# Gate and up products of two feed-forward halves by seven half-sized block products, and all modulation vectors in the first half

## The chip, the cores and the metric

The kernel runs on one core of a Trainium2 chip. The metric is the time of one execution on the device in microseconds (us), median of three runs; lower is better. TensorE (PE) multiplies, VectorE (DVE), ScalarE (ACT) and GpSimd (POOL) work on vectors, and the queue of SyncE (SP) starts the transfers.

## The reference

Two layers of a transformer trunk in float32, on 512 latent tokens and 256 context tokens of width 1024. A layer is a feed-forward half, a mixer (a convolution module in the first layer, windowed attention in the second), and another feed-forward half; the last half has no context tokens. Every part is scaled and shifted by modulation vectors, which come from a condition vector for the latents and one for the context:

```
ml = silu(c) @ mod_w[i] + mod_b[i]              # nine vectors per layer; mc likewise from c_ctx
h  = rmsnorm(s) * norm_g * (1 + scale) + shift
s  = s + 0.5 * gate * ((silu(h @ w_gate) * (h @ w_up)) @ w_down)      # hidden width 2816
```

The change touches the feed-forward halves two (end of layer 0) and three (start of layer 1), both on all 768 tokens, and the place where the modulation vectors are made.

## The kernel before

Activations lie with channels on the partitions: eight tiles `xl[c]` of 128 x 512 (latents) and eight `xc[c]` of 128 x 256 (context). Each float32 operand of a product is split into two parts of a shorter type: ScalarE copies the value into the high part (`whi`, `hhi`, `hidh`), VectorE subtracts it to get the low part (`wlo`, `hlo`, `hidl`). `mm3` (L117 to 125) then issues three matmuls for each 128 x 128 block of weights: high by high, high by low, low by high, all added in PSUM.

`ffn` (L301) does a feed-forward half. It goes through the 22 hidden chunks of 128 in groups of 5, 5, 6 and 6. For each chunk it loads two weight tiles of 128 x 1024 (gate and up; `load`, L105 to 112: one transfer, one copy, one subtraction) and makes two products, each over eight chunks of input channels and in two pieces: 512 latent tokens, and 256 context tokens with 2 more columns that carry the product of the shift (258). `by_rows` (L289) multiplies the result out of PSUM by the row factor `rb`, `shift_cols` (L282) saves the two extra columns, then come silu (L318), the gating (L319) and the split into the hidden parts (L115, L116). After a group, `down` (L292) adds the group's product with the down weights to the activations (L296). In the last group the operands of the next part are made as each chunk is done (`scaled`, L225 and L226).

The root of the mean square is computed with the token sums in a column (L182), three Newton steps on GpSimd (L168 to 177) and a spreading product (L188, L194), after which ScalarE writes `rb` (L218). The products that need it are already in PSUM by then.

The modulation vectors are made in the background of `ffn` on VectorE: `mod_background` (L355) loads one 128 x 1024 tile for each of 8 chunks of a vector (`mraw`) and sums its product with the condition on the free axis (`junk`, L375), one instruction for the latents and one for the context. The first half makes the seven vectors left of layer 0 (56 tiles), the second half the nine of layer 1 (72 tiles).

PSUM has eight banks: three with the tag `a`, two `b`, two `c`, one `st`. Raw weights have three buffers, `whi` and `wlo` three each. The order on each engine is not the order of the code: a list scheduler with a cost model of its own places the instructions, by their place in the program and by when their operands and buffers are free. Once placed, each engine runs its list in order.

Of the kernel before, what the change touches and what calls it, by code (L numbers as in the profile page):

```python
# [10 lines left out]
F32 = mybir.dt.float32  # L11
# [16 lines left out]
TB = T + 2  # L28
# [6 lines left out]
GROUPS = (5, 5, 6, 6)  # L35
DVE_TAPS = ((1, 0), (2, 0), (3, 0), (4, 0))
# [6 lines left out]
# columns of the packed parameters  # L43
# [12 lines left out]
def tile_trunk(ctx: ExitStack, tc, xin, cb, cs, par, modp, modv, gu, dn, pw1, pw2, wqk, wv, wo, bv, rpb, out):  # L56
# [25 lines left out]
    sT = const.tile([P, NC, 32], F32, name="sT")  # L82
    cst = const.tile([P, NC, 2], F32, name="cst")
    nc.sync.dma_start(cst, cs)
# [20 lines left out]
    def load(src, cols=1024):  # L105
        raw = main.tile([P, 1024], F32, tag="raw", name="raw", bufs=3)
# [11 lines left out]
    def mm3(po, w, acts, o, n, first=True, last=True):  # L118
        whi, wlo = w
        k = len(acts)  # L120
        for i, (ah, al) in enumerate(acts):
            s = slice(i * P, (i + 1) * P)
            nc.tensor.matmul(po, lhsT=whi[:, s], rhs=ah[:, o:o + n], start=first and i == 0, stop=False)  # L123
            nc.tensor.matmul(po, lhsT=whi[:, s], rhs=al[:, o:o + n], start=False, stop=False)  # L124
            nc.tensor.matmul(po, lhsT=wlo[:, s], rhs=ah[:, o:o + n], start=False, stop=last and i == k - 1)  # L125

    def h_tiles(i):
        return (main.tile([P, TB], F32R, tag="hhi", name=f"hhi{i}", bufs=8),
                main.tile([P, TB], F32R, tag="hlo", name=f"hlo{i}", bufs=8))

# [14 lines left out]
    def both(ap):  # L145
        return ap.rearrange("p (s c) -> p s c", s=1).broadcast_to([P, 2, NC])

    def finish_mod(l, n, bias=None):
        t = mods[l, n]
        nc.vector.tensor_tensor(t, t, both(pv("mod_b", (l * 9 + n) * 8, 8)), ALU.add)  # L150
        if n % 3 == 1:
            d = derv[l, n] = derived(l, n)
            nc.vector.scalar_tensor_tensor(d, t, 1.0, both(pv("norm_g", (l * 3 + n // 3) * 8, 8)), ALU.add, ALU.mult)
        elif n in (2, 8):
            d = derv[l, n] = derived(l, n)
            nc.vector.tensor_scalar(d, t, 0.5, None, ALU.mult)
        elif n == 5:
            d = derv[l, n] = derived(l, n)
            nc.vector.tensor_tensor(d, t, both(pv("b_pw2" if l == 0 else "b_o")), ALU.mult)

# [1 line left out]
    def newton_rsqrt(sums, k, eps, quick):  # L162
        """1 / sqrt(sums / D + eps) of the columns, from a guess by the exponent."""
# [20 lines left out]
    def spread(y, streams, use):  # L184
        """Token values on partitions to rows on all partitions."""
# [25 lines left out]
    def rms_rows(streams, quick=False):  # L211
# [6 lines left out]
        spread(y, streams, lambda q, o, n: nc.scalar.activation(rb[:, o:o + n], q, AF.Copy))  # L218
# [41 lines left out]
    # products of one unit of weights: (first token, tokens, columns, stream) of each piece; the last  # L260
    # one holds the products of the shift as well
# [38 lines left out]
    def ffn(idx, h, hid, pieces, gate, bg, done, pre=(), tail=None):  # L300
        f0 = 0  # L301
        e = pieces[-1][0] + pieces[-1][1]
        for gi, gn in enumerate(GROUPS):
            hids = []
            for j in range(gn):
                f = f0 + j
                wg, wu = (pre[2 * f + i] if 2 * f + i < len(pre) else load(gu[idx, f, i]) for i in range(2))
# [15 lines left out]
                bg()  # L323
# [15 lines left out]
            for d in range(NC):  # L339
# [4 lines left out]
                if last:  # L344
                    done(d)
                elif d % 3 == 1:
                    bg()
            f0 += gn

# [7 lines left out]
    def mod_background(pool, units):  # L357
# [5 lines left out]
        def step(k):  # L363
            for _ in range(k):
# [8 lines left out]
                for s in range(2):  # L373
# [22 lines left out]
    # ================= layer 0, first half =================  # L396
    with tc.tile_pool(name="start", bufs=1) as hid:
        nc.gpsimd.memset(sT, 0.0)
# [59 lines left out]
    with tc.tile_pool(name="ffn0", bufs=1) as hid:  # L458
        step = mod_background(hid, unit_list(0, range(2, 9)))
        hn = new_h()  # L460
        ffn(0, h, hid, FULL, (0, 2), lambda: step(2),
# [5 lines left out]
    # ================= layer 0, convolution module =================  # L467
    with tc.tile_pool(name="conv", bufs=1) as cv:
# [47 lines left out]
        # taps on the tensor engine: four shifts of 32 channels on the partitions, four such products side by side  # L516
# [19 lines left out]
        # sums over the channels, shifted by the mean of the first 128 of them  # L536
# [87 lines left out]
        ln_out(z, mps, CTX)  # L624
        for d in range(NC):
# [18 lines left out]
        h = new_h()  # L644
        scaled_all(h, derv[0, 7], mods[0, 6])
        rms_rows(BOTH)
        ctx2.close()

    # ================= layer 0, second half; layer 1, first half =================
    with tc.tile_pool(name="ffn1", bufs=1) as hid:  # L650
        step = mod_background(hid, unit_list(1, range(9)))
        hn = new_h()
        ffn(1, h, hid, FULL, (0, 8), lambda: step(3),
            lambda d: scaled_parts(hn, d, BOTH, derv[1, 1], mods[1, 0]))
        rms_rows(BOTH)
        step(99)
        h = hn
        hn = new_h()

        def tail(st):  # L660
            rms_rows((st,), True)
# [279 lines left out]
```

## Time and profile before

| | |
|---|---|
| median of three runs | 2747.97 us (2747.5 to 2748.68) |
| span of the profiled execution, first to last instruction | 2745.9 us |
| TensorE busy | 2700.0 us (98%), 16948 matmuls, as many weight loads |
| VectorE busy | 1673.2 us (61%) |
| ScalarE busy | 822.1 us (30%) |
| transfers | 277.73 MB, mean 101 GB/s |

The profile gives the span alone for its execution, and no other time of it; the median lies 2.07 us above the span. The trace records for each instruction its start, its duration, what it reads and writes, and for an engine that was idle what it waited for. Matmuls overlap, so that their durations do not add up; what one costs in a stream is read from the distance of starts. By the column sums that end each part, half one runs to about 600 us, the convolution module to 897 us, half two to 1449 us, half three to 2020 us and attention to 2361 us.

### The profile page before, as it was taken

The numbers are of one execution on the slowest core, as the hardware profiler recorded it, in microseconds if no ns is written. First come the engines' busy times: TensorE is split into PE (matmuls) and PEld (weight loads), VectorE is DVE, ScalarE is ACT, GpSimd is POOL, SyncE is SP. The second block draws the span as 40 slices with busy tenths as digits, with TensorE's granted clock in tenths as the row PEclk, the third lists the DMA queues.
The fourth block names the chain that finished last, engine by engine and source line by source line (L and its number), as shares of the span: only waits on it lengthen the run. The fifth ranks groups of instructions, "written<-read, shape, count | busy, mean of one in ns | idle before, by whom it ended". The sixth has DMA issues, their size and how long they took to land.

```text
span 2745.9 us, 41215 instructions
## 1 busy us (share of the span) xinstructions
PE 2700.0 (98%) x16948; PEld 2353.4 (86%) x16948; DVE 1673.2 (61%) x3048; ACT 822.1 (30%) x1306; POOL 68.1 (2%) x124
## 2 busy tenths in 40 slices
PE   8999999999989999999999999999999999999997
PEld 4888888888869888888888888888888888999997
DVE  5999533357998999833363433433478576544446
ACT  4212221241236212121242221212346455422224
POOL 0000000011020100000000000000000000000001
PEclk9999999999999999999999999999999999999999
DMA  8565212122435565412121212121242121233223
GB/s 297 163 211 175 88 55 71 56 71 78 127 78 178 168 195 177 158 54 70 58 72 50 75 50 67 61 69 61 80 121 62 58 73 46 74 105 95 88 99 112
DMA packets 95101, 277.73 MB, mean 101 GB/s; under 512 B 11329, under 2 KB 25793, under 8 KB 94657
## 3 DMA queue, kind: packets, MB, share of 16 engines
q1 hardware_dynamic: 94336, 273.52, 31.4%
q8 instruction: 133, 2.18, 0.3%
q0 software_dynamic: 576, 1.57, 0.2%
q14 instruction: 56, 0.45, 0.1%
HBM read 269.09 MB, written 4.38 MB: 100 GB/s over the span
## 4 chain that ended last, share of the span: by engine, by line
PE 93%; DVE 3%; ACT 1%; issue 1%; DMA 1%; POOL 0%; SPq 0%; DVEq 0%; POOLq 0%; ACTq 0%
PE a L125 12%; PE a L123 12%; PE a L124 11%; PE c L123 9%; PE c L125 9%; PE c L124 9%; PE b L125 8%; PE b L124 8%; PE b L123 8%; PE st L793 2%; PE b L784 1%; DVE y L514 1%; PE c L532 1%; PE a L759 1%; PE a L760 1%
## 5 line engine op out<-in xcount | busy, mean ns | idle before, releaser
L110 ACT ACTIVATE whi<-raw 128x1024 fp32r<-128x1024 f32 (+2 forms) x376 | 360.0, 960 | 1437.8 <-PE c L124 1046.0
L111 DVE TENSOR_TENSOR wlo<-raw,whi 128x1024 fp32r<-128x1024 f32 (+2 forms) x376 | 411.8, 1098 | 100.1 <-ACT whi L110 98.1
L125 PE MATMUL a<-hhi,wlo 128*128 128x512 f32 (+2 forms) x1264 | 442.2, 350 | 0.4 <-DVE wlo L111 0.4
L124 PE MATMUL a<-hlo,whi 128*128 128x512 f32 (+2 forms) x1264 | 440.3, 348 | 0.0
L123 PE MATMUL a<-hhi,whi 128*128 128x512 f32 (+2 forms) x1264 | 440.3, 349 | 0.0
L123 PE MATMUL c<-hhi,whi 128*128 128x258 f32 (+2 forms) x1456 | 428.6, 295 | 4.3 <-ACT hhi L115 2.1
L125 PE MATMUL c<-hhi,wlo 128*128 128x258 f32 (+2 forms) x1456 | 429.2, 295 | 0.0
L124 PE MATMUL c<-hlo,whi 128*128 128x258 f32 (+2 forms) x1456 | 427.1, 294 | 0.5 <-DVE hlo L116 0.5
L375 DVE SCALAR_TENSOR_TENSOR junk<-mraw,sbc 128x1024 f32<-128x1024 f32 x256 | 312.7, 1221 | 3.8 <-ACT sbc L360 2.0
L123 PEld LDWEIGHTS c<-hhi,whi 128*128 128x128 f32 x1456 | 275.7, 190 | 15.6 <-ACT hhi L115 2.7
L123 PE MATMUL b<-hhi,whi 128*128 128x512 f32 (+2 forms) x800 | 280.3, 350 | 6.0 <-ACT hhi L225 3.4
L124 PEld LDWEIGHTS c<-hlo,whi 128*128 128x128 f32 x1456 | 276.7, 190 | 10.8 <-DVE hlo L116 1.3
L125 PE MATMUL b<-hhi,wlo 128*128 128x512 f32 (+2 forms) x800 | 280.9, 351 | 0.5 <-DVE wlo L111 0.5
L125 PEld LDWEIGHTS c<-hhi,wlo 128*128 128x128 f32 x1456 | 275.1, 189 | 7.1 <-issue 1.0
L124 PE MATMUL b<-hlo,whi 128*128 128x512 f32 (+2 forms) x800 | 280.1, 350 | 0.5 <-DVE hlo L226 0.5
L125 PEld LDWEIGHTS a<-hhi,wlo 128*128 128x128 f32 x1264 | 237.8, 188 | 34.0 <-issue 1.1
L124 PEld LDWEIGHTS a<-hlo,whi 128*128 128x128 f32 x1264 | 238.1, 188 | 32.9 <-issue 0.2
L123 PEld LDWEIGHTS a<-hhi,whi 128*128 128x128 f32 x1264 | 238.0, 188 | 31.3 <-issue 0.8
L123 PEld LDWEIGHTS b<-hhi,whi 128*128 128x128 f32 x800 | 151.0, 189 | 29.6 <-ACT hhi L225 3.6
L124 PEld LDWEIGHTS b<-hlo,whi 128*128 128x128 f32 x800 | 151.0, 189 | 22.8 <-DVE hlo L226 1.0
L125 PEld LDWEIGHTS b<-hhi,wlo 128*128 128x128 f32 x800 | 150.9, 189 | 22.2 <-DVE wlo L111 1.0
L124 PE MATMUL a<-hidl,whi 128*128 128x512 f32 (+1 forms) x431 | 162.7, 377 | 0.0
(202 smaller groups left out, 4169.8 us busy)
## 6 DMA issues: line engine op xcount, KB each, us to landing
raw<-in_gu SPq DMA_DIRECT2D x176, 512.0 KB
mraw<-in_modv SPq DMA_DIRECT2D x128, 512.0 KB
raw<-in_dn SPq DMA_DIRECT2D x80, 384.0 KB
raw<-in_dn SPq DMA_DIRECT2D x64, 320.0 KB
raw<-in_pw SPq DMA_DIRECT2D x24, 512.0 KB
us<-v SPq DMA_DIRECT2D x64, 142.0 KB
mraw<-in_modp SPq DMA_DIRECT2D x16, 512.0 KB
raw<-in_wqk SPq DMA_DIRECT2D x16, 512.0 KB
```

The lines of the kernel that those rows point to most:

```text
L110: nc.scalar.activation(hi[:, :cols], raw[:, :cols], AF.Copy)
L111: nc.vector.tensor_tensor(lo[:, :cols], raw[:, :cols], hi[:, :cols].bitcast(F32), ALU.subtract)
L123: nc.tensor.matmul(po, lhsT=whi[:, s], rhs=ah[:, o:o + n], start=first and i == 0, stop=False)
L124: nc.tensor.matmul(po, lhsT=whi[:, s], rhs=al[:, o:o + n], start=False, stop=False)
L125: nc.tensor.matmul(po, lhsT=wlo[:, s], rhs=ah[:, o:o + n], start=False, stop=last and i == k - 1)
L375: nc.vector.scalar_tensor_tensor(junk, raw, 1.0, sbc[:, s, :], ALU.mult, ALU.mult, accum_out=m[:, s, c:c + 1])
L514: nc.vector.scalar_tensor_tensor(yo, u[:, k:k + n], w, yo, ALU.mult, ALU.add)
L532: nc.tensor.matmul(po[ST * g:ST * g + ST, e:e + PIECE], lhsT=dg[:, 4 * m + g], rhs=t[:, g, 4 * m:4 * m + PIECE], start=m == 0, stop=m == 7)
L759: nc.tensor.matmul(so, lhsT=qq[:, qsl], rhs=kk[:, ks], start=True, stop=False)
L760: nc.tensor.matmul(so, lhsT=ql[:, qsl], rhs=kk[:, ks], start=False, stop=True)
L784: nc.tensor.transpose(pt[:, i * P:(i + 1) * P], p[:, i * P:(i + 1) * P], ident)
L793: nc.tensor.matmul(po[64 * a:64 * a + 64, :P], lhsT=v[:, c0:c0 + 64], rhs=PT[a][:, i * P:(i + 1) * P], start=i == 0, stop=i == 3)
```

## The change

In the halves two and three the gate and up products are no longer made block by block. The 768 tokens are taken as two blocks of 384 (256 latents and 128 context tokens each, with two columns for the shift: 386), the eight chunks of input channels as four even and four odd ones, the hidden chunks as pairs. The product of a pair is then one of 2 x 2 blocks by 2 x 2 blocks, and is made with seven block products instead of eight (Winograd's form): four sums of the weight quarters, four of the activation quarters, and additions of the products.

- `s_weights` loads the two tiles of a pair, makes the four weight sums on VectorE (new L398 to L402) and splits seven quarters in four pieces: quarters (1, 2), (6, 5) and (7, 3) together, (4) alone. Each takes one of the three `whi` and `wlo` buffers.
- `s_unit` makes the seven products (L417), each of 4 x 3 matmuls of 386 columns, in the order 1, 2, 6, 5, 7, 3, 4. Products 1, 6, 7 and 4 add up in one bank (`a`), 5 and 3 in another (`c`), 2 stands alone (`b`). ScalarE saves three sums in between (`kept`, L422) and writes one row (L439), VectorE writes three rows (L429, L435, L437) into a tile in SBUF.
- The row factor (L487, L498), silu (L489) and gating (L500) then work on these tiles.
- `s_prepare` makes the activation quarters and their sums for two chunks of channels at a time: four scalings on ScalarE into `sg`, two copies on GpSimd, seven quarters split in four pieces, four subtractions into `tu`. The tiles `sg` and `tu` have one buffer each. The quarters take 16 slots with the tag `h` and 12 with the tag `hx`; the input of the convolution's last product, `z`, fills all 16 of `h`.
- `s_ffn` runs over pairs in groups of 2, 2, 2, 2 and 3, so that there are 40 down steps of a half in place of 32. The down products read the same columns as before.
- All 128 modulation tiles are made in half one; for four vectors of layer 1 the context is left out, since the last half has no context tokens.
- Raw weights have four buffers.

```diff
-GROUPS = (5, 5, 6, 6)            # still used by halves one and four
+PAIRS = (2, 2, 2, 2, 3)
+    def s_weights(src, pool):
+        raws = []
+        for i in range(2):
+            raw = main.tile([P, 1024], F32, tag="raw", name="raw", bufs=4)
+            nc.sync.dma_start(raw, src[i])
+            raws.append(raw)
+        q = [raws[0][:, :512], raws[0][:, 512:], raws[1][:, 512:], raws[1][:, :512]]
...
+        def parts_of(t, names):
+            n = 512 * len(names)
+            hi = main.tile([P, 1024], F32R, tag="whi", name="whi", bufs=3)
+            lo = main.tile([P, 1024], F32R, tag="wlo", name="wlo", bufs=3)
+            split(hi[:, :n], lo[:, :n], t[:, :n])
...
+        parts_of(raws[0], (1, 2))
+        nc.vector.tensor_tensor(s1, q[2], q[3], ALU.add)
+        nc.vector.tensor_tensor(s2, s1, q[0], ALU.subtract)
+        parts_of(s12, (6, 5))
+        nc.vector.tensor_tensor(s3, q[0], q[2], ALU.subtract)
+        nc.vector.tensor_tensor(s4, q[1], s2, ALU.subtract)
+        parts_of(s34, (7, 3))
+        parts_of(raws[1], (4,))
+    def s_unit(src, hs, pool, row):
+        made = s_weights(src, pool)
+        def product(name, p, first):
+            hi, lo, o = made[name]
+            for j in range(4):
+                k = slice(o + j * P, o + j * P + P)
+                ah, al = hs[name][j]
+                for i, (a, b) in enumerate(((hi, ah), (hi, al), (lo, ah))):
+                    nc.tensor.matmul(p, lhsT=a[:, k], rhs=b, ...)
+        x, y, z = (bank(t)[:, :SB] for t in "abc")
+        product(1, x, True)
+        a = kept(x)
+        product(2, y, True)
+        nc.vector.tensor_tensor(row[:, 0, 0], y, a, ALU.add)
+        product(6, x, False)
+        b = kept(x)
+        product(5, z, True)
+        d = kept(z)
+        product(7, x, False)
+        nc.vector.tensor_tensor(row[:, 1, 1], x, d, ALU.add)
+        product(3, z, False)
+        nc.vector.tensor_tensor(row[:, 0, 1], z, b, ALU.add)
+        product(4, x, False)
+        nc.scalar.activation(row[:, 1, 0], x, AF.Copy)
+    def s_prepare(j, hs, pool, A, B):
+        sx = s_row(pool, "sg")                               # bufs=1
+        tt = s_row(pool, "tu").rearrange("p a b n -> p (a b) n")
...
+        split(*hs[1][j], sx[:, 0, 0])
+        two((2, 3), sx[:, 1])
+        nc.vector.tensor_tensor(tt[:, 0], sx[:, 0, 1], sx[:, 0, 0], ALU.subtract)
+        nc.vector.tensor_tensor(tt[:, 1], sx[:, 1, 1], tt[:, 0], ALU.subtract)
+        two((5, 6), tt[:, :2])
+        nc.vector.tensor_tensor(tt[:, 2], sx[:, 1, 1], sx[:, 0, 1], ALU.subtract)
+        nc.vector.tensor_tensor(tt[:, 3], sx[:, 1, 0], tt[:, 1], ALU.subtract)
+        two((7, 4), tt[:, 2:])
-        step = mod_background(hid, unit_list(0, range(2, 9)))
+        step = mod_background(hid, unit_list(0, range(2, 9)) + unit_list(1, range(9)))
-        ffn(0, h, hid, FULL, (0, 2), lambda: step(2), ...)
+        ffn(0, h, hid, FULL, (0, 2), step, ...)              # bg(3) per hidden chunk, bg(2) per down step
-        h = new_h()
-        scaled_all(h, derv[0, 7], mods[0, 6])
-        rms_rows(BOTH)
-        step = mod_background(hid, unit_list(1, range(9)))
-        ffn(1, h, hid, FULL, (0, 8), lambda: step(3), ...)
+            if d % 2:                                        # inside the loop of the last conv product
+                s_prepare(d // 2, hs, hid, derv[0, 7], mods[0, 6])
+        s_rows(BOTH)
+        s_ffn(1, hs, hid, (0, 8), done=done)
+        s_ffn(2, hs2, hid, (1, 2), tail=tail)
```

Three places of the new order. The first is TensorE in half two. Before, from one weight tile to the next (names: `h..3` is a channel chunk, `whi_13233` a gate tile, `whi_13239` the up tile of the same hidden chunk, `whi_13363` the gate tile of the next):

```order
L123 MATMUL c_13295<-hhi7_8133,whi_13233 128x258
L124 MATMUL c_13295<-hlo7_8134,whi_13233 128x258
L125 MATMUL c_13295<-hhi7_8133,wlo_13234 128x258
L123 MATMUL c_13320<-hhi0_8119,whi_13239 128x258
L124 MATMUL c_13320<-hlo0_8120,whi_13239 128x258
L125 MATMUL c_13320<-hhi0_8119,wlo_13240 128x258
```

Now, at the end of product 6 of a gate tile pair (`whi_9648` holds quarters 6 and 5, `whi_9654` 7 and 3, `whi_9771` 1 and 2 of the up weights that come next):

```order
L417 MATMUL a_9662<-h_8518,whi_9648 128x386
L417 MATMUL a_9662<-h_8519,whi_9648 128x386
L417 MATMUL a_9662<-h_8518,wlo_9649 128x386
L417 MATMUL a_9791<-h_7840,whi_9771 128x386
L417 MATMUL a_9791<-h_7841,whi_9771 128x386
L417 MATMUL b_9792<-hx_7844,whi_9771 128x386
L417 MATMUL b_9792<-hx_7845,whi_9771 128x386
L417 MATMUL a_9662<-hx_7856,whi_9654 128x386
```

Four matmuls with the next weights stand between product 6 and product 7, in 22 units of the 44. The second place is ScalarE beside it (`kept_9704` saves the bank after product 6, `kept_9718` after product 5):

```order
L422 ACTIVATE kept_9677<-a_9662 128x386
L115 ACTIVATE hid_9620<-tu_9367 128x768
L115 ACTIVATE whi_9658<-raw_9638 128x512
L115 ACTIVATE whi_9771<-raw_9765 128x1024
L422 ACTIVATE kept_9704<-a_9662 128x386
L422 ACTIVATE kept_9718<-c_9664 128x386
```

The copy of the next weights stands ahead of the two that save the banks. Its buffer is that of `whi_9648`, the third before it.

The third place is VectorE where half two begins, after the convolution's last product. Before (`x7`, `xc7`: the last channel chunk; `hlo`: low parts of the operand; `junk`: modulation):

```order
L636 TENSOR_TENSOR t_7924<-x7_82,t_7978 128x4x8x8
L640 TENSOR_TENSOR xc7_95<-xc7_95,t_8006 128x256
L116 TENSOR_TENSOR hlo4_8025<-mod0_6_2647,hhi4_8024 128x2
L226 SCALAR_TENSOR_TENSOR hlo5_8027<-xc5_93,dv0_7_3625,hhi5_8026 128x256
L375 SCALAR_TENSOR_TENSOR junk_8722,mod1_1_8577<-mraw_8718,sbc_8116 128x1024
L116 TENSOR_TENSOR hlo5_8027<-mod0_6_2647,hhi5_8026 128x2
L226 SCALAR_TENSOR_TENSOR hlo6_8029<-xc6_94,dv0_7_3625,hhi6_8028 128x256
```

Now (`sg` and `tu` with a number are the single buffers of one call of `s_prepare`: 7832 the first call, 8056 the second; `h` and `hx` the low parts):

```order
L116 TENSOR_TENSOR h_7841<-sg_7832,h_7840 128x386
L469 TENSOR_TENSOR tu_8057<-sg_8056 128x386
L470 TENSOR_TENSOR tu_8057<-sg_8056,tu_8057 128x386
L472 TENSOR_TENSOR tu_8057<-sg_8056 128x386
L473 TENSOR_TENSOR tu_8057<-sg_8056,tu_8057 128x386
L116 TENSOR_TENSOR wlo_8579<-s34_8565,whi_8578 128x1024
L822 TENSOR_TENSOR xc7_92<-xc7_92,t_8492 128x256
L221 TENSOR_TENSOR acc_80<-acc_80,t_8496 128x512
L116 TENSOR_TENSOR h_7841<-sg_8056,h_7840 128x386
```

The second, third and fourth call of `s_prepare` stand one behind the other after the convolution's last product, the first call's tile being free only when its first quarter has a slot of `h`. From the first row shown to the low parts of quarters 5 and 6 of the last call there are 32 rows on VectorE.

## Rows read from the trace of the kernel before

**Rows 1.** page, busy time of each engine: us, share of the span, instructions

```profile
PE 2700.0 (98%) x16948; PEld 2353.4 (86%) x16948; DVE 1673.2 (61%) x3048; ACT 822.1 (30%) x1306; POOL 68.1 (2%) x124
```

**Rows 2.** page, chain that ended last, by engine

```profile
PE 93%; DVE 3%; ACT 1%; issue 1%; DMA 1%; POOL 0%; SPq 0%; DVEq 0%; POOLq 0%; ACTq 0%
```

**Rows 3.** timeline, TensorE: start us, us, operation; the first of each stretch

```profile
1302.57 0.29 PE L123 MATMUL c<-hhi,whi 128*128 128x258 f32 x1
...
1308.33 0.39 PE L123 MATMUL b<-hhi,whi 128*128 128x512 f32 x1
...
1313.91 0.40 PE L123 MATMUL a<-hhi,whi 128*128 128x512 f32 x1
```

**Rows 4.** groups of instructions by shape: busy us, mean ns, idle before

```profile
L375 DVE SCALAR_TENSOR_TENSOR junk<-mraw,sbc 128x1024 f32<-128x1024 f32 x256 | 312.7, 1221 | 3.8 <-ACT sbc L360 2.0
...
L111 DVE TENSOR_TENSOR wlo<-raw,whi 128x1024 fp32r<-128x1024 f32 x232 | 283.7, 1223 | 86.3 <-ACT whi L110 84.6
...
L125 PEld LDWEIGHTS c<-hhi,wlo 128*128 128x128 f32 x1456 | 275.1, 189 | 7.1 <-issue 1.0
L110 ACT ACTIVATE whi<-raw 128x1024 fp32r<-128x1024 f32 x232 | 245.7, 1060 | 982.3 <-PE c L124 733.8 <-PE b L124 76.4 <-PE a L124 75.7
...
L319 DVE SCALAR_TENSOR_TENSOR tu<-tu,bcol,sg 128x512 f32<-128x512 f32 x88 | 66.2, 752 | 7.5 <-ACT whi L110 0.5 <-ACT sg L318 0.4
L116 DVE TENSOR_TENSOR hidl<-tu,hidh 128x768 fp32r<-128x768 f32 x66 | 63.0, 954 | 2.1 <-ACT hidh L115 1.6
...
L786 ACT ACTIVATE pts<-b 128x512 f32<-128x512 f32 x64 | 37.6, 596 | 56.7 <-PE b L784 56.5
...
L319 DVE SCALAR_TENSOR_TENSOR tu<-tu,bcol,sg 128x256 f32<-128x256 f32 x66 | 31.7, 480 | 0.0
L289 DVE TENSOR_TENSOR sg<-c,rb 128x256 f32<-128x256 f32 x74 | 31.4, 425 | 107.9 <-PE c L125 106.2 <-ACT rb L218 1.7
...
L209 DVE TENSOR_TENSOR acc<-acc,t 128x512 f32<-128x512 f32 x42 | 29.0, 692 | 13.1 <-ACT t L208 12.9
...
L375 DVE DVE_READ_ACCUMULATOR junk<-mraw,sbc 128x1 f32 x256 | 21.9, 85 | 0.0
```

**Rows 5.** windows: stretch, its us, busy of PE, PEld, DVE, ACT, POOL, clock, DMA share, GB/s

```profile
100.00:300.00 200.00, 200.00 (x1143) 175.44 (x1143) 185.24 (x323) 39.77 (x51) 0.00 (x0) 1.00 0.56 181
300.00:500.00 200.00, 200.00 (x1144) 175.26 (x1143) 78.22 (x123) 42.63 (x53) 0.00 (x0) 1.00 0.20 64
1450.00:1500.00 50.00, 50.00 (x285) 43.42 (x285) 20.84 (x35) 12.93 (x17) 2.57 (x13) 1.00 0.15 49
1500.00:1900.00 400.00, 400.00 (x2283) 350.60 (x2282) 154.12 (x243) 80.25 (x102) 0.00 (x0) 1.00 0.20 63
1990.00:2050.00 60.00, 57.83 (x299) 48.25 (x298) 46.25 (x94) 24.99 (x39) 3.28 (x6) 1.00 0.36 110
```

**Rows 6.** timeline, TensorE, where the second feed-forward half begins

```profile
919.03 0.39 PE L123 MATMUL c<-hhi,whi 128*128 128x258 f32 x1 [2.10 <-DVE bcol L282]
...
920.44 0.42 PE L124 MATMUL c<-hlo,whi 128*128 128x258 f32 x1
...
923.45 0.36 PE L123 MATMUL c<-hhi,whi 128*128 128x258 f32 x1
```

**Rows 7.** timeline, GpSimd, the reciprocal roots of that place

```profile
904.04 1.05 POOL L177 TENSOR_TENSOR nwt<-nwt 128x6 f32<-128x6 f32 x1
905.17 0.20 POOL L170 TENSOR_TENSOR nwt<-nwt 128x6 f32<-128x6 f32 x1
```

**Rows 8.** waits of TensorE from 560 to 2050 us: total, times, longest

```profile
PE c L123 <- DVE bcol L282: 2.1, 1, 2.1
PE b L724 <- ACT hhi L252: 1.5, 1, 1.5
```

More of the change, by code (lines that the diff above doesn't have):

```diff
@@ L122, in mm3, with slot @@
             s = slice(i * P, (i + 1) * P)
-            nc.tensor.matmul(po, lhsT=whi[:, s], rhs=ah[:, o:o + n], start=first and i == 0, stop=False)
-            nc.tensor.matmul(po, lhsT=whi[:, s], rhs=al[:, o:o + n], start=False, stop=False)
-            nc.tensor.matmul(po, lhsT=wlo[:, s], rhs=ah[:, o:o + n], start=False, stop=last and i == k - 1)
+            if o is not None:
+                ah, al = ah[:, o:o + n], al[:, o:o + n]
+            nc.tensor.matmul(po, lhsT=whi[:, s], rhs=ah, start=first and i == 0, stop=False)
+            nc.tensor.matmul(po, lhsT=whi[:, s], rhs=al, start=False, stop=False)
+            nc.tensor.matmul(po, lhsT=wlo[:, s], rhs=ah, start=False, stop=last and i == k - 1)
+    def slot(pool=None):
+        if pool is None:
+            return main.tile([P, TB], F32R, tag="h", name="h", bufs=2 * NC)
+        return pool.tile([P, TB], F32R, tag="hx", name="hx", bufs=12)
     def h_tiles(i):
-        return (main.tile([P, TB], F32R, tag="hhi", name=f"hhi{i}", bufs=8),
-                main.tile([P, TB], F32R, tag="hlo", name=f"hlo{i}", bufs=8))
+        return slot(), slot()
     mods = {}
@@ L306, in ffn @@
                 f = f0 + j
-                wg, wu = (pre[2 * f + i] if 2 * f + i < len(pre) else load(gu[idx, f, i]) for i in range(2))
+                wg, wu = (pre[2 * f + i] if 2 * f + i < len(pre) else load(gu[idx // 3, f, i]) for i in range(2))
                 hh = hid.tile([P, T], F32R, tag="hidh", name="hidh", bufs=6)
@@ new lines, in s_unit, with kept @@
+    def s_unit(src, hs, pool, row):
[6 more added lines that the diff above has]
+                for i, (a, b) in enumerate(((hi, ah), (hi, al), (lo, ah))):
+                    nc.tensor.matmul(p, lhsT=a[:, k], rhs=b, start=first and j == 0 and i == 0,
+                                     stop=j == 3 and i == 2, skip_group_check=True)
+        def kept(p):
+            t = pool.tile([P, SB], F32, tag="kept", name="kept", bufs=3)
+            nc.scalar.activation(t, p, AF.Copy)
+            return t
+        x, y, z = (bank(t)[:, :SB] for t in "abc")
[13 more added lines that the diff above has]
+        nc.scalar.activation(row[:, 1, 0], x, AF.Copy)
@@ L372, in step @@
                 m = mods[l, n]
-                for s in range(2):
+                for s in range(mod_streams(l, n)):
                     junk = pool.tile([P, 1024], F32, tag="junk", name="junk", bufs=1)
@@ L624, in tile_trunk @@
         ln_out(z, mps, CTX)
+        ctx2.close()
+    with tc.tile_pool(name="ffn12", bufs=1) as hid:
+        hs = {}
         for d in range(NC):
@@ L905, in _layout @@
     gate, up, down = (i[k].reshape(4, *i[k].shape[2:]) for k in ("ffn_w_gate", "ffn_w_up", "ffn_w_down"))
-    g["gu"] = np.stack([np.stack([_tiles(gate[k]), _tiles(up[k])], axis=1) for k in range(4)])
+    g["gu"] = np.stack([np.stack([_tiles(gate[k]), _tiles(up[k])], axis=1) for k in (0, 3)])
+    g["gs"] = np.stack([np.stack([_quarters(gate[k]), _quarters(up[k])], axis=1) for k in (1, 2)])
     g["dn"] = np.stack([_tiles(down[k]) for k in range(4)])
```

147 lines of the change are left out of this document (117 added, 30 removed).

## The prediction

> **What bounds the kernel now.** I read the busy times first, then the chain of waits, then the timeline of TensorE, then the windows. TensorE is busy for 2700.0 of 2745.9 us [rows 1], and the chain that ended last lies on it for 93% [rows 2]. Busy TensorE is not TensorE at its peak, so the reader should look at the distance of starts: from 1302.57 to 1308.33 us stand 48 matmuls of 258 columns, 0.1200 us each, and from there to 1313.91 us 24 of 512 columns, 0.2325 us each [rows 3]. The cost follows the columns: 254 more take 0.1125 us more, 0.000443 us per column. In halves two and three TensorE is busy for all of the stretch from 1500 to 1900 us, with the clock at 1.00 (2.4 GHz) [rows 5]. So the time there is a number of columns, and taking columns away shortens it, as long as the other engines keep up. From 1500 to 1900 us VectorE is busy for 154 of 400 us and ScalarE for 80 [rows 5]: there is room, but the change uses most of it.
>
> **TensorE, what goes and what comes.** A half has 22 hidden chunks, 2 products each, 8 channel chunks, 3 matmuls, in two pieces: 1056 matmuls of 512 columns and 1056 of 258. In two halves that is 2112 x (0.2325 + 0.1200) = 744.5 us. Now a half has 11 pairs, 2 units each, 7 products of 4 x 3 matmuls of 386 columns, in two halves 3696. On the line through the two measured points one takes 0.1200 + 128 x 0.000443 = 0.1767 us, together 653.1 us. The difference is -91.4 us, or 33.8 us for a pair before and 29.7 us now. The down products read the same columns in two runs in place of one. No row shows that form; I take it at 0, between 0 and 5% of the 371 us that 2 x 528 x (0.2325 + 0.1190) us make, 19 us.
>
> The weight loads speak against this sum. A load takes 189 ns [rows 4], longer than the 177 ns that I give to a matmul of 386 columns, and the loads are busy for 86% of the span [rows 1]. The Trainium skill (Perfetto Trace Analysis, Identifying the Most-Contended Engine) says to judge TensorE's headroom by the busy share of weight loads and not by that of matmuls. By that the new matmuls would cost their loads, 698.5 us in place of 653.1. The trace speaks against it: 48 matmuls with a load of 189 ns each start every 120 ns [rows 3, 4], so loads overlap one another.
>
> **VectorE in a pair.** From the rows of the same shapes (386 columns between 0.425 and 0.692 us, so 0.56) [rows 4]: six low parts of 1024 columns and two of 512, 8.7 us; eight weight sums of 512, 5.5; six rows out of PSUM, 3.4; four row-factor products of 768, 3.8; gating, 2 x (0.752 + 0.480) = 2.5; two hidden low parts, 1.9. That is 25.8 us in 29.7 us of TensorE: 87%, where the kernel before has 39% [rows 5]. It fits, but with little slack, and nothing on it is background work that could wait.
>
> **The wait in a pair.** The order shows a place where TensorE must stop. The weights' three buffers are used in turn by four pieces, so the first piece of the next unit takes the buffer of quarters 6 and 5 and can be copied only when both products are done. In the 22 units where product 5 comes ahead of product 6, four matmuls that want this copy stand directly behind product 6, and on ScalarE the copy stands ahead of the one that saves the bank for product 7. So TensorE waits for one copy of 1024 columns, 1.06 us [rows 4], and its start. Twenty of these units lie outside the two transitions below: 20 x 1.1 = +22 us. Bounds: 0, if the buffer is free early enough, and 20 x (1.06 + 1.22) = 46 us, if the low part is waited for as well. In the other 22 units product 5 ends after product 6 and ten of its matmuls (1.8 us) cover the save, and product 7 (2.1 us) covers the copy; I take 0.
>
> **The transitions.** Where half two begins, `s_prepare` is called four times with single buffers, and the first call waits for a slot that the convolution's last product holds. So three calls run one after the other behind that product. From the first low part to the low parts of quarters 5 and 6 of the last call VectorE has 32 instructions: sixteen of 386 columns (9.0 us), eight of 772 and one of 768 (8.6), one of 1024 (1.2), three of 512 (2.1), and small ones of 1.1, in all 22 us. TensorE has for that time 24 matmuls of 256 columns (2.9 us) and three products (6.4 us), and then stops, some 13 us; one more for the first copy, 14. Before, the same place cost a wait of 2.10 us and a spell at 0.5 of the clock (1.2 GHz), with starts 0.215 us apart instead of 0.120 from 920.44 to 923.45 us [rows 6]. Such a spell of 3.4 us loses 1.7 us. I take two spells: 14 + 3.4 - 3.8 = +14 us, bounds 0 and 25.
>
> GpSimd's root steps stand in this path too: they took 1.05 us each while VectorE worked and 0.20 us when it stood idle [rows 7]. The Trainium skill (SBUF — State Buffer, Who interferes with whom) says that a VectorE instruction with two inputs in SBUF contends with a GpSimd instruction that reads SBUF, and the two durations agree with it. The upper bound holds the ten steps at the longer time.
>
> Where half three begins, the first three calls have slots early and only the last is late. Before, TensorE did not wait there: 50.00 of 50 us [rows 5]. From the last update to the low parts of quarters 5 and 6 VectorE now has 12.5 us by the same rows, TensorE four products' worth, 8 us, and the spreading product then waits for GpSimd, some 1.5 us: +6, and one spell, +8 us; bounds 0 and 14. In the eight inner group ends of these halves the last hidden parts are late by about what three prepared down steps cover; I take 0.5 us each, +4, bounds 0 and 16.
>
> **The modulation vectors.** Half one gets 72 more tiles: its instructions go from 112 to 224, each 1.221 + 0.085 us [rows 4], 293 us in all. With the 39% of VectorE's other work over some 560 us (218 us) it is busy for 91%. From 100 to 300 us it was busy for 185 of 200 us with the same mix, and TensorE for all 200, with the transfers at 0.56 [rows 5]. Queue SP holds the same alternation of weights and tiles as there, only for longer. So 0, with 10 us as the price if the cover fails at the group ends; the last of these instructions stands in the last group, ahead of the convolution. What half two loses of them gives TensorE nothing, except at its start, where they stood in the path, which is in the 3.8 us.
>
> **Sum.** -91.4 + 22 + 14 + 8 + 4 = -43.4 us, so a span of 2702.5 us. The median of the runs shown lies 2.07 us above the span of before (2747.97 to 2745.9), and I add the same: 2704.6, say 2705 us.
>
> **Rivals.**
> - *The waits do not come, or half of them.* For it: VectorE at 93% left TensorE without a wait [rows 5]. Against: the order puts the copy right behind product 6. Without the 22 and the 4 us: 2679 us; chance 0.17.
> - *The clock falls at each wait.* For it: the wait of 2.10 us was followed by 1.2 GHz [rows 6]. Against: a wait of 1.5 us where attention starts (L724) [rows 8] left the clock at 1.00 in the stretch to 2050 us [rows 5]. Twenty spells at 1.7 us: 2705 + 34 = 2739 us; chance 0.10. The Trainium skill (TensorE: Matmul & The Clock Gate, A second HAM failure mode: psum-queue depth-cycling) tells of short idle times between groups of matmuls that made the clock swing; no run here shows it yet.
> - *Slower: VectorE cannot keep up in either unit of a pair.* Its list has waits in it (rows that need a product stand ahead of low parts that TensorE needs), and at 87% it cannot catch up. The price is 1.06 + 1.22 us in each of 44 units, 100 us in place of 22: 2705 + 78 = 2783 us. It decides from 1.6 us per unit on: 44 x 1.6 - 22 = 48 us, which brings 2705 to 2753. Against: the down steps in between give it 4.2 us of TensorE for two updates and a low part of 512 columns, 1.9 us. Chance 0.11.
> - *Each new matmul costs its weight load:* 3696 x 0.189 = 698.5 us in place of 653.1, so 45 us come back: 2750 us, no change. For it: the load is longer than the new matmul [rows 4]. Against: the starts 120 ns apart [rows 3]. Chance 0.03. It is what the Trainium skill's rule on weight loads would make of this kernel (Perfetto Trace Analysis, above).
>
> **Chances.** The forecast 0.59, the rivals 0.17, 0.10, 0.11 and 0.03. Its own range, from the bounds of the pair and of the first transition, is 2684 to 2732 us. The range for all reaches to the first two rivals and leaves the others out: 2676 to 2740 us. A measurement of this kernel can tell 0.2% (5.5 us) from no change. Faster by more than that (under 2742.5): 0.85; within it 0.05; slower 0.10.
>
> **What would show it.** Starts of 386-column matmuls 0.177 us apart; 22 waits of about 1.1 us of TensorE for `whi` of the new split; a gap of some 14 us where half two begins, and of 6 us at half three; TensorE without waits in half one, VectorE over 90% to about 520 us. Wrong would be: starts above 0.185 us, waits in all units, the clock at half inside the halves, or TensorE waiting in half one.

## The result, and the profile after

The changed kernel takes 2699.39 us (median of 4 runs, 2698.88 to 2700.21), beside 2747.8 us for the kernel before on the same chip (4 runs, 2747.5 to 2748.68): a ratio of 0.9822, 95% interval 0.9808 to 0.9836. The forecast was 2705 us, the range 2676 to 2740 us. The profiled execution has a span of 2698.4 us at a mean granted clock of 0.992.

The busy times and the chain by engine answer to [rows 1, 2]. TensorE's busy time has gone from 2700.0 to 2629.3 us, VectorE's up by 232 us, and the chain has moved a little from TensorE to VectorE.

```profile
PE 2629.3 (97%) x16420; PEld 2358.1 (87%) x16420; DVE 1905.2 (71%) x3268; ACT 985.1 (37%) x1601; POOL 77.5 (3%) x140
...
PE 90%; DVE 4%; issue 2%; ACT 2%; DMA 1%; POOL 1%; SPq 0%; DVEq 0%; POOLq 0%; ACTq 0%
```

The timeline of TensorE in half two shows the new stream and its stop (start us, us, operation, in brackets the idle time before and what ended it). From 1027.03 to 1029.15 us stand the 12 matmuls of product 5, then the 12 of product 6, the last at 1031.08.

```profile
1027.03 0.52 PE L417 MATMUL c<-hx,whi 128*128 128x386 f32 x2
...
1029.15 0.51 PE L417 MATMUL a<-hx,whi 128*128 128x386 f32 x2
...
1031.08 0.34 PE L417 MATMUL a<-h,wlo 128*128 128x386 f32 x1
1032.44 0.62 PE L417 MATMUL a<-h,whi 128*128 128x386 f32 x2 [1.02 <-ACT whi L115]
1032.89 0.51 PE L417 MATMUL b<-hx,whi 128*128 128x386 f32 x2
1033.24 0.52 PE L417 MATMUL a<-hx,whi 128*128 128x386 f32 x2
```

Twelve matmuls in 2.12 us are 0.1767 us each, the value read off the line through [rows 3]. A weight load still takes 190 ns, longer than that (groups of instructions: busy us, mean ns, idle before):

```profile
L417 PEld LDWEIGHTS a<-h,whi 128*128 128x128 f32 x880 | 160.0, 190 | 30.9 <-ACT whi L115 26.2
```

ScalarE's timeline at the same place shows what TensorE waits for: the copy of the next unit's first weights starts as product 6 ends, and the save of product 6's bank stands behind it.

```profile
1027.39 0.63 ACT L115 ACTIVATE whi<-raw 128x512 fp32r<-128x512 f32 x1
1031.33 1.06 ACT L115 ACTIVATE whi<-raw 128x1024 fp32r<-128x1024 f32 x1 [3.31 <-issue]
1032.29 0.48 ACT L422 ACTIVATE kept<-a 128x386 f32<-128x386 f32 x1
```

In the waits of TensorE from 905 to 1960 us this is nearly the only row (total us, times, longest):

```profile
PE a L417 <- ACT whi L115: 19.5, 21, 1.0
PE st L206 <- DVE t L200: 1.3, 1, 1.3
```

The windows answer to [rows 5] (same columns); the two from 905 to 1960 us leave out only the start of half three, and the last two are the places where halves two and three begin.

```profile
100.00:300.00 200.00, 200.00 (x1146) 175.74 (x1145) 187.86 (x328) 39.76 (x51) 0.00 (x0) 1.00 0.59 192
300.00:500.00 200.00, 200.00 (x1145) 175.50 (x1144) 186.76 (x328) 42.65 (x53) 0.00 (x0) 1.00 0.64 213
...
905.00:1425.00 520.00, 509.76 (x2881) 482.48 (x2880) 355.61 (x504) 206.04 (x322) 4.91 (x8) 1.00 0.22 67
1436.00:1960.00 524.00, 513.47 (x2889) 483.10 (x2888) 352.58 (x499) 198.41 (x302) 0.60 (x3) 1.00 0.23 73
1500.00:1900.00 400.00, 391.73 (x2216) 372.83 (x2216) 266.35 (x373) 146.73 (x225) 0.00 (x0) 1.00 0.22 69
...
880.00:910.00 30.00, 23.14 (x93) 17.06 (x92) 22.86 (x36) 20.47 (x35) 8.18 (x18) 0.77 0.11 35
1420.00:1450.00 30.00, 27.72 (x147) 25.84 (x146) 23.77 (x36) 17.82 (x29) 7.59 (x15) 0.94 0.11 36
```

Half one holds VectorE at 93% without a wait of TensorE. Inside half three the clock is 1.00 and the idle time 8.27 us, all of it the waits above. Where half two begins, TensorE is busy for 23.14 of 30 us at a mean clock of 0.77; its rows there answer to [rows 6]:

```profile
884.23 0.45 PE L417 MATMUL a<-h,whi 128*128 128x386 f32 x1 [1.75 <-ACT h L115]
...
888.11 0.69 PE L417 MATMUL b<-hx,whi 128*128 128x386 f32 x1 [0.78 <-DVE hx L116]
...
897.36 2.04 PE L206 MATMUL st<-t,ones 128*128 128x512 f32 x2 [1.83 <-DVE t L200]
...
899.52 0.53 PE L417 MATMUL b<-h,whi 128*128 128x386 f32 x1
...
902.45 0.45 PE L417 MATMUL c<-h,whi 128*128 128x386 f32 x1 [0.52 <-DVE h L116]
```

A matmul of 386 columns shows 0.34 us at clock 1.00 and 0.53 us at 0.50 (1.2 GHz). The long form stands from 886.9 to 900.6 us, after TensorE had worked in short pieces between waits; it ends while TensorE still waits for operands.

To size the steps I add up, over the timeline, the distance from each start to the next less the time that its columns take (0.1767, 0.2325 and 0.1185 us for 386, 512 and 256), and call the rest the lost time. It counts waits, restarts and half clock together, and is good to about 1 us for a place.

### The profile page after: what moved, and what is told of

It reads as the page before. It is cut to its first block, busy times and chain, and to the rows that moved or that the text cites. A ratio compares the mean times of both kernels' runs of the same rounds, so it can differ in the third digit from the quotient of the medians.

```text
span 2698.4 us, 40901 instructions
## 1 busy us (share of the span) xinstructions
PE 2629.3 (97%) x16420; PEld 2358.1 (87%) x16420; DVE 1905.2 (71%) x3268; ACT 985.1 (37%) x1601; POOL 77.5 (3%) x140
## 4 chain that ended last, share of the span: by engine, by line
PE 90%; DVE 4%; issue 2%; ACT 2%; DMA 1%; POOL 1%; SPq 0%; DVEq 0%; POOLq 0%; ACTq 0%
PE a L417 13%; PE a L125 8%; PE a L127 8%; PE a L126 8%; PE c L417 6%; PE c L125 6%; PE c L126 6%; PE c L127 6%; PE b L125 5%; PE b L126 5%; PE b L127 5%; PE b L417 3%; PE st L975 2%; PE b L966 1%; DVE y L691 1%
## 5 line engine op out<-in xcount | busy, mean ns | idle before, releaser
L110 ACT ACTIVATE whi<-raw 128x1024 fp32r<-128x1024 f32 (+3 forms) x304 | 270.0, 891 | 862.2 <-PE c L126 454.3
L111 DVE TENSOR_TENSOR wlo<-raw,whi 128x1024 fp32r<-128x1024 f32 (+3 forms) x304 | 306.0, 1009 | 89.8 <-ACT whi L110 87.7
L125 PE MATMUL a<-h,whi 128*128 128x512 f32 (+2 forms) x826 | 270.0, 328 | 1.1 <-DVE sg L301 1.1
L127 PE MATMUL a<-h,wlo 128*128 128x512 f32 (+2 forms) x826 | 269.0, 326 | 0.9 <-DVE wlo L111 0.9
L126 PE MATMUL a<-h,whi 128*128 128x512 f32 (+2 forms) x826 | 269.0, 326 | 0.0
L417 PE MATMUL a<-h,whi 128*128 128x386 f32 x880 | 234.8, 345 | 21.9 <-ACT whi L115 19.5
L125 PE MATMUL c<-h,whi 128*128 128x258 f32 (+2 forms) x768 | 233.1, 306 | 1.2 <-ACT h L115 1.1
L126 PE MATMUL c<-h,whi 128*128 128x258 f32 (+2 forms) x768 | 233.3, 305 | 0.6 <-DVE h L116 0.6
L127 PE MATMUL c<-h,wlo 128*128 128x258 f32 (+2 forms) x768 | 232.4, 303 | 0.0
L417 PEld LDWEIGHTS a<-h,whi 128*128 128x128 f32 x880 | 160.0, 190 | 30.9 <-ACT whi L115 26.2
L125 PE MATMUL b<-h,whi 128*128 128x512 f32 (+2 forms) x550 | 181.7, 330 | 5.3 <-ACT h L237 3.4
L126 PE MATMUL b<-h,whi 128*128 128x512 f32 (+2 forms) x550 | 180.8, 329 | 0.5 <-DVE h L238 0.5
L125 PEld LDWEIGHTS a<-h,whi 128*128 128x128 f32 x826 | 155.8, 189 | 16.9 <-DVE sg L301 2.0
L126 PEld LDWEIGHTS a<-h,whi 128*128 128x128 f32 x826 | 156.2, 189 | 14.1 <-issue 0.8
L126 PEld LDWEIGHTS c<-h,whi 128*128 128x128 f32 x768 | 145.3, 189 | 8.6 <-DVE h L116 1.2
L125 PEld LDWEIGHTS c<-h,whi 128*128 128x128 f32 x768 | 144.1, 188 | 9.6 <-ACT h L115 1.5
L417 PE MATMUL a<-h,wlo 128*128 128x386 f32 x440 | 149.4, 340 | 0.0
```

The lines of the kernel that those rows point to most:

```text
L110: nc.scalar.activation(hi[:, :cols], raw[:, :cols], AF.Copy)
L111: nc.vector.tensor_tensor(lo[:, :cols], raw[:, :cols], hi[:, :cols].bitcast(F32), ALU.subtract)
L125: nc.tensor.matmul(po, lhsT=whi[:, s], rhs=ah, start=first and i == 0, stop=False)
L126: nc.tensor.matmul(po, lhsT=whi[:, s], rhs=al, start=False, stop=False)
L127: nc.tensor.matmul(po, lhsT=wlo[:, s], rhs=ah, start=False, stop=last and i == k - 1)
L417: nc.tensor.matmul(p, lhsT=a[:, k], rhs=b, start=first and j == 0 and i == 0, stop=j == 3 and i == 2, skip_group_check=True)
```

## Experiments

All times are medians beside the kernel before on the same chip (2748.1 to 2748.5 us there). Where two kernels were not run together, their ratios to it are compared.

**1. Three raw buffers again.** Edit, in `load` and `s_weights`:

```
-        raw = main.tile([P, 1024], F32, tag="raw", name="raw", bufs=4)
+        raw = main.tile([P, 1024], F32, tag="raw", name="raw", bufs=3)
```

> The changed kernel with three raw weight buffers in place of four (undoes that part of the change). Theory: the transfers land long before they are used, so 2699 us, within 4 us; the waits for the copy behind product 6 stay, 21 times about 1 us. Rival: half a unit of prefetch is gone, and TensorE or VectorE waits for transfers, at 1 us or more in each of 44 units: 2740 us or more, with DMA named in the waits.

2695.87 us, ratio 0.9809 (0.9796 to 0.9823). In halves two and three no transfer is waited for, and the waits for the copy stay:

```profile
PE a L417 <- ACT whi L115: 18.5, 20, 1.0
```

The fourth buffer buys nothing. The 3.5 us less are not told from nothing, since the two kernels did not run together and their intervals overlap. In the traces they gather in small steps: about 1 us before half two, 1.2 us in halves two and three, where one wait for the copy is gone, and about 1 us behind them; the rest of the cause is open.

**2. Quarter 4 in a buffer of its own.** On top of the first edit, in `parts_of` (the low part likewise, as `w4l`):

```
-            hi = main.tile([P, 1024], F32R, tag="whi", name="whi", bufs=3)
+            hi = pool.tile([P, 512], F32R, tag="w4h", name="w4h", bufs=1) if n == 512 else main.tile(...)
```

> Three raw buffers, and the fourth piece of a unit's weights (quarter 4 alone) in a buffer of its own, so that the ring of three turns once per unit and the first piece of the next unit takes the buffer of quarters 1 and 2, which is free early. Theory: the 21 waits of 0.8 to 1.0 us behind product 6 came from that ring; they go, and with their restart (about 1.1 us each in the distances of starts) 22 us with them: 2676 us if three raw buffers cost nothing. Rival: the copy was only named last, and the save of the bank (0.48 us) or a low part on VectorE is next: half or more of the waits stay, 2688 us or more.

2674.17 us, ratio 0.9730 (0.9717 to 0.9743), 21.7 us under experiment 1 on the same chip. From 905 to 1400 us the view of waits is empty, and the window that had 8.27 us of idle time has none:

```profile
1500.00:1900.00 400.00, 400.00 (x2237) 380.55 (x2236) 273.24 (x378) 155.77 (x234) 0.00 (x0) 1.00 0.22 70
```

In the place of the copy, ScalarE's timeline has only the save behind product 6, and TensorE doesn't notice it:

```profile
1028.30 0.85 ACT L115 ACTIVATE hid<-tu 128x768 fp32r<-128x768 f32 x1 [0.56 <-DVE tu L500]
1031.05 0.49 ACT L422 ACTIVATE kept<-a 128x386 f32<-128x386 f32 x1 [1.91 <-PE a L417]
```

So the ring of three made the waits, as the forecast read it from the order, and they cost what it said.

**3. Early slots for the first operand chunks.** In `s_prepare`:

```
-            ones_ = [slot() for _ in range(2)]
+            ones_ = [slot(of) for _ in range(2)]
-        two((7, 4), tt[:, 2:])
+        two((7, 4), tt[:, 2:], None if j == 1 else of)      # `two` takes the pool
```

> The changed kernel, with the first two operand chunks of a half in the 12 slots that the convolution does not hold (the last two parts of chunk 1 go to the others instead), so that the first preparation and most of the second run before the convolution's last product. Theory: VectorE's list behind that product is shorter by 8 us of its 22, and TensorE stops that much less: 2691 us (2688 to 2695), and the spell at half clock is shorter than 13.65 us. Rival: the column sums, GpSimd's root steps and the spreading product set the end of the gap, so at most 3 us are saved: 2696 us or more.

2689.68 us, ratio 0.9786 (0.9773 to 0.9799): 9.7 us less than the kernel after, and 6.2 us less than experiment 1, which ran on the same chip. The window where half two begins is now

```profile
880.00:910.00 30.00, 27.26 (x135) 25.13 (x134) 23.98 (x37) 17.86 (x30) 8.18 (x15) 0.89 0.11 36
```

and the lost time of that place falls from 15.5 to 9.3 us, by the 6.2 us that the comparison on one chip gives. One wait for the copy is gone here too (20, 18.5 us), which is 1 us of the rest; the other 2.5 us are less than the intervals of two chips tell apart. So VectorE's list sets the end of the gap and the rival is refuted, but the gain is nearer to 6 us than to the 8 that were expected.

**4. The modulation vectors alone,** on the kernel before:

```
-        step = mod_background(hid, unit_list(0, range(2, 9)))
+        step = mod_background(hid, unit_list(0, range(2, 9)) + unit_list(1, range(9)))
...
-        ffn(1, h, hid, FULL, (0, 8), lambda: step(3),
+        ffn(1, h, hid, FULL, (0, 8), nothing,
```

> The kernel before, with all modulation vectors made in the first half and nothing else changed. Theory: VectorE has the room in half one (over 90% busy there, TensorE never waiting), and half two loses only the wait and the half-clock spell at its start, so 2744 to 2748 us. Rival: the cover fails at the group ends of half one, and the end of half one or the convolution is later by 10 us: 2758 us.

2744.59 us, ratio 0.9986 (0.9977 to 0.9995). VectorE is busy for 93% from 300 to 500 us and for 95% from there to 600 us, and TensorE is never idle there, although this kernel makes all 256 sums in half one where the change leaves 32 out; where half two begins TensorE is busy for 60.00 of 60 us, where it had the wait and the spell of [rows 6].

```profile
300.00:500.00 200.00, 200.00 (x1143) 175.29 (x1142) 185.92 (x327) 42.64 (x53) 0.00 (x0) 1.00 0.58 191
500.00:600.00 100.00, 100.00 (x574) 87.86 (x573) 95.16 (x176) 34.56 (x63) 0.00 (x0) 1.00 0.52 167
880.00:940.00 60.00, 60.00 (x339) 51.98 (x338) 32.39 (x63) 23.54 (x43) 3.53 (x13) 1.00 0.17 55
```

**5. Experiments 2 and 3 together.**

> The two edits together: quarter 4 in a buffer of its own with three raw buffers, and the early slots for the first two operand chunks. Theory: they act at different places, so their gains add: 2674.2 less the 9.7 us that the slots gave alone, 2664.5 us, within 4 us. Rival: with the ring changed the first weights come later into the transition, so that half or less of the 9.7 us is left: 2669 us or more.

2666.25 us, ratio 0.9702 (0.9687 to 0.9716). The gains add to within 2 us, whether the slots are taken at 9.7 us (2664.5 us) or at 6.2 (2668 us). From 1000 to 1350 us TensorE is busy for all of the time; what is lost lies in the transitions, 7.8 us at half two and 7.0 at half three.

**6 and 7. More work for VectorE,** on experiment 2. In `s_weights` (five times in the second):

```
-        nc.vector.tensor_tensor(s3, q[0], q[2], ALU.subtract)
+        for _ in range(3): nc.vector.tensor_tensor(s3, q[0], q[2], ALU.subtract)
```

> On the kernel with quarter 4 in its own buffer: the third sum of each unit is computed three times in place of once (same result), two more VectorE instructions of 512 columns, 0.6 us each, in all 44 units, 53 us of VectorE work. Theory: TensorE's stream sets the time, and a pair's VectorE list grows from 25.8 to 28.3 us of 29.7: 2674 to 2680 us. Rival (the one that forecast a slower kernel): waits inside VectorE's list leave no slack, and each unit is later by what is added, 44 times 1.2 us: 2727 us.

> As the one with the sum computed three times, but five times: four more instructions in each unit, 106 us of VectorE work, a pair's list 30.7 us. Theory: now the list is longer than TensorE's 29.7 us and VectorE sets the time of a pair, 22 times 1 us more and something for the waits in the list: 2690 to 2715 us. Rival 1: the down steps between the pairs give it a lead, nothing is seen: under 2682 us. Rival 2: no slack at all, 44 times 2.4 us: 2780 us.

2678.16 us, ratio 0.9746 (0.9731 to 0.9760), and 2679.55 us, ratio 0.9751 (0.9736 to 0.9765). The second expectation fails: the 106 us of added work (VectorE's busy time goes from 1904.3 to 2004.1 us) cost 5.4 us beside experiment 2; the two ran on different chips, and their intervals allow for 0 to 13 us. TensorE doesn't wait in the window

```profile
1000.00:1350.00 350.00, 350.00 (x1990) 337.00 (x1989) 276.92 (x400) 136.75 (x208) 0.00 (x0) 1.00 0.21 68
```

The reason is in VectorE's timeline of the second kernel (start us, us):

```profile
1005.95 0.68 DVE L401 TENSOR_TENSOR s<-raw 128x512 f32<-128x512 f32 x1
1006.55 0.68 DVE L402 TENSOR_TENSOR s<-raw,s 128x512 f32<-128x512 f32 x1
1007.15 0.68 DVE L401 TENSOR_TENSOR s<-raw 128x512 f32<-128x512 f32 x1
```

Instructions that follow one another without a wait start 0.60 us apart where each shows 0.68 us. VectorE's durations overlap by some 0.08 us and do not add up, as TensorE's do not. By the distances of starts (1.14, 0.60 and 0.47 us for 1024, 512 and 386 columns, 0.88 for 768, 0.66 and 0.40 for the two parts of the gating) the list of a pair is 23.1 us and not 25.8, and with eight sums more it is 27.9 us, still less than TensorE's 29.7. So the list never got longer than TensorE's, and this experiment doesn't show what happens when it does. What the added work costs is lost in the transitions, which go from 14.4 and 6.9 us in experiment 2 to 17.5 and 10.8 us.

**8. One product less,** on experiment 2: `product(4, x, False)` is left out.

> On the kernel with quarter 4 in its own buffer: the matmuls of the last of the seven products are left out in all units (the lower left block of each unit then lacks that product, and the output is not the reference's). 528 matmuls of 386 columns less, 93.3 us at 0.1767 us each. Theory: TensorE needs 25.4 us for a pair then, VectorE 25.8, so VectorE becomes the bound and some of the gain is lost: 2584 to 2610 us. Rival: matmuls cost their weight load, 0.189 us, so 99.8 us go and VectorE hides: 2574 us. Rival 2: VectorE was near its limit already, and half or less of the 93 us comes: 2627 us or more.

2601.13 us, ratio 0.9464 (0.9449 to 0.9480), 73 us less of the 93.3. The time lies in the expected interval, but not for the reason given. VectorE is busy for 74%, and TensorE waits at the inner group ends for the last hidden parts, in the stretch from 905 to 1400 us four times:

```profile
PE a L125 <- ACT hid L115: 3.5, 2, 1.7
PE b L125 <- ACT hid L115: 3.5, 2, 1.7
PE a L417 <- ACT h L115: 1.7, 1, 1.7
```

Over both halves eight such waits are 14.0 of the 21.0 us more of lost time. One of the eight was followed by half clock inside half two (mean 0.83 from 1040 to 1050 us). It is the way from the last product to the down step that is late, not the sum of VectorE's work.

**9. Matmuls that fill the gap,** on the kernel after, at the end of `s_prepare`:

```
+        if j == 3 and B is mods[0, 6]:
+            for jj in range(4):
+                pf = pst()[:, :SB]
+                for _ in range(6):
+                    nc.tensor.matmul(pf, lhsT=hs[1][jj][0][:, :P], rhs=hs[1][jj][0], start=True, stop=True)
```

> The changed kernel, with 24 more matmuls of 386 columns (4.2 us at full clock) into an unused bank where half two begins, six for each operand chunk, so that TensorE stands still less while VectorE prepares the operands. Theory: VectorE's list sets the end of this gap, so the matmuls fill time that was idle or at half clock anyway: 2699 to 2703 us, whether or not the clock stays up. Rival: the half-clock spell of 13.65 us is itself a cost of up to 6.8 us; if the fill keeps the clock at 1.00, the time falls to 2696 us or less, and if it doesn't, the fill costs its 4 to 8 us in full: 2703 us or more.

2701.76 us (2699.49 to 2703.43), ratio 0.9830 (0.9816 to 0.9843). The clock still fell (0.83 from 880 to 910 us), so the price of the spell itself is not settled. Lost time and the fill's 4.2 us together make 15.8 us there, beside 15.5 without the fill: it went where time was lost anyway. The 2.4 us more than the kernel after, which ran on another chip, are less than the intervals tell apart; in the trace half three, whose order changed with the edit, loses 10.7 us, and 7.3 in the kernel after.

**10 to 12. GpSimd out of the transitions.** In the kernel after, GpSimd's small copy of the shift columns took 2.19 us for two at 888.12 us and the last pair stood behind the root steps; in experiment 5, at half three, two took

```profile
1400.56 4.53 POOL L453 COPY sg<-mod 128x4 f32<-128x4 f32 x2 [15.24 <-DVE tu L473]
```

The copy moves to VectorE in the kernel after (10) and in experiment 5 (11); in 12 the root steps move too:

```
-            nc.gpsimd.tensor_copy(sx[:, r, :, BLK:], ...)
+            nc.vector.tensor_copy(sx[:, r, :, BLK:], ...)
-        rms_rows(streams, use=use)
+        rms_rows(streams, True, use=use)      # 12 only
```

> The changed kernel, with the small copy of the shift columns (128x4, line 453) on VectorE in place of GpSimd. In the trace of the changed kernel the last preparation of half two has its copy queued on GpSimd behind the root steps (from 890.40 to 896.2 us, copy at 896.16). Theory: GpSimd's queue sets the end of that gap; 3 to 6 us go there and 1 to 2 at half three: 2691 to 2696 us. Rival: VectorE's list sets the end whatever GpSimd does, and it gets 16 more small instructions: 2698 us or more.

> The kernel with quarter 4 in its own buffer and the early slots, and the small copy on VectorE. In its trace the chain goes over this copy in both transitions (3.3 us for two at half two, 4.42 us for one at half three). Theory: 4 to 7 us go: 2659 to 2662 us. Rival: VectorE's list or the root steps behind it are next: 2664 us or more.

> As the one before, with the root steps of the row factors on VectorE too, ten instructions of some 0.16 us in place of GpSimd's 6 us, so that GpSimd has no part in the transitions. Theory: another 1 to 3 us, since the spreading product then waits for nothing: 2657 to 2660 us. Rival: the roots were hidden behind the first products, nothing changes within 1 us, or VectorE's list grows by 2 us and TensorE waits that much longer: 2662 us or more.

2699.09 us, ratio 0.9823 (0.9810 to 0.9837); 2668.37 us, ratio 0.9709 (0.9696 to 0.9722); 2663.81 us, ratio 0.9694 (0.9680 to 0.9707). My theory of the copy falls: moving it alone gains nothing. In experiment 10 the root steps take its place. The last of them stands on GpSimd at 894.48 us, VectorE waits for it, and the low parts of the last preparation are queued behind:

```profile
894.71 0.96 DVE L200 TENSOR_TENSOR t<-ident,nwt 128x768 f32<-128x768 f32 x1 [1.63 <-POOL nwt L189]
```

With the root on VectorE as well, 4.6 us go against experiment 11 on the same chip, 2.9 of them where half two begins (lost time 9.7 to 6.8 us). Experiment 12 is the fastest kernel here, 3.1% under the kernel before; against experiment 5, which ran beside another set of runs, its lead of 2.4 us is less than the intervals tell apart.

## Why the forecast held, step by step

- *The stream, -91.4 us.* Held: 0.1767 us per matmul, and the down steps in two runs start 0.233 us apart at 512 columns, so the strided form costs nothing, as taken.

```profile
983.84 0.39 PE L126 MATMUL a<-hid,whi 128*128 128x512 f32 x1
...
986.17 0.39 PE L127 MATMUL a<-hid,wlo 128*128 128x512 f32 x1
```

- *The copy behind product 6, +22 us.* Held: 21 waits, with their restarts 22.8 us of lost time, and 21.7 us when the ring is changed (experiment 2).
- *The start of half two, +14 us.* Mis-sized: the lost time is 14.4 us where it was 4.4, so +10. The cause held (three preparations behind the convolution's last product; experiment 3), the make-up did not: I had 14 us of standing still and two short spells, and the trace has 5.9 us of idle time, without the wait counted above, and one spell of 13.65 us at half clock. TensorE works slowly for part of the time in which it would have stood, so the two seem not to add; experiment 9 could not settle that, since the clock fell there too. What I left at a bound, GpSimd's root steps in this path, is real: 2.9 us of lost time (experiments 11 and 12).
- *The start of half three, +8 us.* About 6 us, by the same mechanism.
- *VectorE's 25.8 us in a pair, 87%.* Misread: durations were added that overlap. By the distances of starts it is 23.1 us, 78% (experiments 6 and 7). The 22 us of the first transition are added the same way, and would be some 2.6 us less for 32 rows; that the list still took from 879.11 to about 902.4 us is due to waits inside it, 3.5 us, of which 1.79 us are for GpSimd's last root step.
- *Group ends, +4 us.* Mis-sized: about nothing. They come with one product less (experiment 8), so the cover was there, but only by a few us for each group.
- *The modulation vectors, 0, and 3.8 us less where half two begins.* Held: -3.9 us alone (experiment 4).

The terms as measured make -91.4 + 22.8 + 10 + 6 = -52.6 us; the span fell by 47.5. By the column sums, 49.2 us went between the last one ahead of half two (at 813.7 us before, 813.6 now) and the first one at the end of half three (1988.7 and 1939.4). The stretch behind that is 1.8 us longer, all of it in half four (354.7 us before, 356.5 now), where TensorE doesn't wait more; its cause is open. Most of the 3.4 us left is the stream of before, which was cheaper than taken: from 930 to 1430 us of the kernel before, the starts behind matmuls of 512 columns average 0.231 us and not 0.2325, for 2112 of them some 3 us (an estimate).

That the sum came within 4 us of the span is in part luck. The three places were taken too high by 4, 2 and 4 us, and the stream's saving too high by about 3, with 1.8 us in half four that were not forecast; the errors have both signs.

Of the rivals, the fall of the clock at each wait is refuted: 21 idle times of 0.8 to 1.0 us left it at 1.00 from 905 to 1425 and from 1436 to 1960 us. Within halves two and three of this kernel it fell only in the transitions, where several waits follow one another within 20 us. The Trainium skill (TensorE: Matmul & The Clock Gate, A second HAM failure mode: psum-queue depth-cycling) tells of such swings at short idle times; inside the halves this trace does not show them. A longer wait can do it: in experiment 8 one of eight waits of 1.7 us was followed by 1.2 GHz inside half two.

The price of a weight load for each new matmul is refuted by the starts, 0.177 us apart at loads of 0.190 us. The rule of the Trainium skill (Perfetto Trace Analysis, Identifying the Most-Contended Engine) that takes the busy share of weight loads as the measure would leave 5% in experiment 2, where loads are busy for 380.55 of 400 us. The trace does not agree: TensorE is busy for all of the 400 us there and waits for nothing. And one product less takes 94 us out of its stream (73 us of time, and 21 us more of lost time), which are the 93.3 us of its columns and not the 99.8 us of its loads.

That VectorE cannot keep up is refuted too, and by more than I had thought: 87% of a pair looked close, but it was 78%, and four more instructions in each unit cost 5.4 us in all. The slower kernel deserved less than its 0.11.

## What to carry to other kernels

Fewer columns in a stream bound by TensorE come back as computed from the start distances; what has to be found by hand is where the new operand work ends late. Read from the order which buffer of a ring the next unit's first copy takes: a ring whose period isn't the unit's puts a wait into every other unit, and one small buffer of its own removed 22 us here. Judge a second engine's room by the distances of its starts too: added durations made VectorE look 2.7 us fuller in a pair than it was. And look for its price where the prepared work of a stage begins.

## What was not expected of the hardware

A copy of 128x4 elements on GpSimd, 0.31 us for two when VectorE was mostly idle (at 879.80 us), took up to 4.53 us for two beside VectorE's sums and subtractions. VectorE's instructions start 0.08 us earlier than the durations before them end. And a spell of 13.65 us at half clock was not followed by a longer gap than forecast with two of 3.4 us: the first operands that TensorE waits for after it, at 902.45 us, come from VectorE.
